# Branch projections by seven products on half-size blocks, with the two sides of PSUM exchanged

## The chip, the cores and the metric

The kernel runs on one core of one Trainium2 chip. The metric is the device time of one execution in microseconds (us), lower is better. A profiled execution also has a span, from its first instruction to its last.

## What is computed

One step of a hybrid decoder layer for 512 prompt tokens and 32 sample tokens (544 columns in all), in fp32. Three branches work on the projected input: a short convolution, a state-space recurrence, a cross-attention. What matters here is how they are merged:

```python
conv_out = (cb * conv * jax.nn.silu(cz)) @ p['w_conv_out']
...
ys = jax.nn.gelu(ys * jax.nn.silu(sz))
ssm_out = (ys @ p['w_glu_a']) * jax.nn.sigmoid(ys @ p['w_glu_b'])
...
attn_out = (o * jax.nn.silu(az)) @ p['w_attn_out']
g = jax.nn.sigmoid(gpre).reshape(bsz, L, N_BRANCH, D_MODEL)
merged = g[:, :, 0] * conv_out + g[:, :, 1] * ssm_out + g[:, :, 2] * attn_out
return x + merged @ p['w_out'], new_conv, new_re, new_im
```

The four matrices `w_attn_out`, `w_conv_out`, `w_glu_a` and `w_glu_b` are 1024 x 2048 each. The four products with them, each of 1024 x 2048 by 1024 x 544, are the branch projections, and they are all that the change rewrites.

## The kernel before, in words

Activations lie transposed: channels on the 128 partitions, the T = 544 tokens along the free dimension, in two halves of NH = 272. A matrix product in fp32 is made of three products in the faster format F32R: every operand is split into a high part `hi` (a copy on ScalarE, ACT, L91) and a low part `lo` (source minus high part, on VectorE, DVE, L92), and hi*hi, hi*lo and lo*hi are summed in PSUM. The helper `split` (L90 to L92) records both instructions, so most splits of the kernel have these two lines in the profile and differ by their tiles.

The plain product is `proj` (L127). It takes 256 columns of a weight matrix through `stream` (L94), which loads blocks of 512 rows by 256 columns (512 KB, queue of SyncE, SP; pool `wraw`, four buffers), splits each (pool `whl`, two buffers), and issues 48 matmuls per block: 2 column tiles of 128, 4 row tiles, 3 products, 2 halves of the tokens. With 1024 rows a call has 2 blocks and 96 matmuls. After each block `tick` runs a step of background work, if there is any.

The stage ahead of the branches computes the gates (L1059 to L1066) with `winograd` (L1009): Winograd's form of Strassen's algorithm. The weights are halved along rows and columns and the activations along channels and tokens, and seven products of halves take the place of eight. The blocks of weights that go into the products are sums and differences: three on DVE (L1038, L1045, L1048), one on GpSimd (POOL, L1044). The blocks of activations, the factors `XT`, are made and split once, in the stage before. A product is 24 matmuls; its split weights lie in `shi` and `slo` with three buffers each. Results are added up partly in PSUM (products that accumulate on an earlier one) and partly on DVE (L1050, L1052, L1055). The gates go to DRAM (`gt_d`), by POOL's queue.

The branch stage (L1070 to L1122) first opens the standard pools again (`open_std`, L1070), then loads the three branch inputs from DRAM (`od_d`, `cv_d`, `gz_d`) with `branch_input` (L1081): eight pieces of 272 KB by ACT's queue, each split on arrival into `preh` and `prel`. Then come three loops over 8 groups of 256 columns. For attention, DVE multiplies the result out of PSUM with the gate into `mg` (L1102). For the convolution, DVE multiplies (L1108) and POOL adds to `mg` (L1109). For the GLU there are two `proj` calls per group, a sigmoid on ACT (L1118), two multiplications on DVE (L1114, L1119) and POOL's addition (L1120). Gates are loaded by ACT's queue (L1093).

After it (L1128) the sixteen tiles `mg` are split into `mh` and `ml` and multiplied with `w_out`, in the same manner with `proj`.

Order on the engines: the program is recorded in the order of the code, and the Tile framework then orders each engine's instructions by its own schedule (the `TileContext` of the launch has `schedule_with_timeline_sim=True`), so an instruction can run ahead of earlier code when its inputs are there. In the gate stage the difference L1045 of one call runs ahead of the addition L1055 of the call before. Each engine then works its list in order. A pool with `reuse_waits="tile"` lets a new tile wait for just those older tiles whose memory it takes.

## Time and profile before

| | us |
|---|---|
| median of 3 runs | 2225.22 |
| the runs | 2224.7 to 2228.82 |
| the profiled execution's own time | 2227.26 |
| its span | 2225.5 |
| TensorE matmuls busy | 2126.1 |
| DVE busy | 1107.5 |
| ACT busy | 708.8 |
| POOL busy | 481.3 |

PE is TensorE's matmul, PEld its weight load, which overlaps it. Matmuls are pipelined, so a matmul's own duration (some 0.29 us) is longer than the time from one start to the next. "mean ns" is the mean duration of one instruction; "idle before" is time in which the engine waited ahead of these instructions, with what released it. Lines as L92 are lines of the kernel.

### The profile page before, as it was taken

Reading aid. Unit: us, or ns where it says so; the run is one execution under the profiler, and the core shown is the slowest. Engines: PE = TensorE matmul, PEld = TensorE weight load, DVE = VectorE, ACT = ScalarE, POOL = GpSimd, SP = SyncE. Lnnn points to the kernel's source line nnn. Section 1 sums busy time; section 2 is a strip of 40 time slices with the busy share of each in tenths; the row PEclk is TensorE's granted clock in tenths of the full one; section 3 lists DMA queues with packets and bytes.
Section 4 is the critical chain, followed back from the end, with each engine's and each line's share of the span. In section 5 each row is a group of like instructions: output and inputs, shape, how many; then the busy total and the mean of one; then the engine's idle time right before and its main releaser. Section 6 shows DMA issues by size and latency. Waiting matters only on the chain.

```text
span 2225.5 us, 39522 instructions
## 1 busy us (share of the span) xinstructions
PE 2126.1 (96%) x16962; PEld 2095.3 (94%) x16962; DVE 1107.5 (50%) x1623; ACT 708.8 (32%) x1014; POOL 481.3 (22%) x336
## 2 busy tenths in 40 slices
PE   3989999999999999989899999999899999999996
PEld 3989999999999998889799999999899999999996
DVE  4534598423334443266567677677544433334232
ACT  4122221223233333223344444444322112223332
POOL 0198510740100002144212111111000210011221
PEclk9999999999999999999899999999999999999998
DMA  6565133344243445543333333334454433327232
GB/s 140 123 126 107 59 96 96 109 109 130 87 143 125 132 162 176 176 145 107 107 126 129 121 124 134 126 125 134 163 190 146 136 121 120 106 86 178 84 96 81
DMA packets 262483, 277.00 MB, mean 124 GB/s; under 512 B 59146, under 2 KB 242018, under 8 KB 260292
## 3 DMA queue, kind: packets, MB, share of 16 engines
q1 hardware_dynamic: 214144, 204.11, 30.9%
q10 hardware_dynamic: 39460, 37.62, 6.0%
q0 software_dynamic: 8704, 32.75, 4.0%
q8 instruction: 133, 2.18, 0.4%
q14 instruction: 42, 0.34, 0.1%
HBM read 241.96 MB, written 31.96 MB: 123 GB/s over the span
## 4 chain that ended last, share of the span: by engine, by line
PE 76%; DVE 5%; DMA 2%; issue 1%; ACTq 1%; ACT 1%; POOL 0%; DVEq 0%; SPq 0%; POOLq 0%
PE mmps L137 15%; PE mmps L143 15%; PE mmps L140 15%; PE pA L1032 13%; PE pB L1032 9%; PE mmps L824 1%; PE mmps L823 1%; PE mmps L825 1%; DVE wlo L92 1%; PE aux L618 1%; PE aux L875 1%; PE dsc L863 1%; DMA stage<-od_d 1%; PE aux L779 1%; PE aux L616 1%
## 5 line engine op out<-in xcount | busy, mean ns | idle before, releaser
L92 DVE TENSOR_TENSOR wlo<-raw,whi 128x1024 fp32r<-128x1024 f32 x256 | 351.2, 1373 | 594.7 <-ACT whi L91 583.5
L91 ACT ACTIVATE whi<-raw 128x1024 fp32r<-128x1024 f32 x256 | 271.2, 1060 | 841.3 <-PE mmps L140 726.7
L143 PE MATMUL mmps<-xh,wlo 128*128 128x272 f32 x2048 | 428.8, 291 | 10.7 <-DVE wlo L92 10.5
L137 PE MATMUL mmps<-xh,whi 128*128 128x272 f32 x2048 | 431.7, 292 | 3.1 <-DVE gate L980 2.2
L140 PE MATMUL mmps<-xl,whi 128*128 128x272 f32 x2048 | 430.7, 290 | 0.0
L143 PEld LDWEIGHTS mmps<-xh,wlo 128*128 128x128 f32 x2048 | 322.7, 189 | 18.3 <-DVE wlo L92 12.4
L140 PEld LDWEIGHTS mmps<-xl,whi 128*128 128x128 f32 x2048 | 325.9, 190 | 4.2 <-issue 4.1
L137 PEld LDWEIGHTS mmps<-xh,whi 128*128 128x128 f32 x2048 | 322.8, 190 | 6.0 <-DVE gate L980 2.4
L92 DVE TENSOR_TENSOR slo<-sraw,shi 128x1024 fp32r<-128x1024 f32 x120 | 191.2, 1593 | 83.0 <-ACT shi L91 83.0
L137 PE MATMUL mmps<-preh,whi 128*128 128x272 f32 x1024 | 213.9, 291 | 10.0 <-ACT preh L91 7.9
L140 PE MATMUL mmps<-prel,whi 128*128 128x272 f32 x1024 | 212.8, 289 | 0.5 <-DVE prel L92 0.5
L143 PE MATMUL mmps<-preh,wlo 128*128 128x272 f32 x1024 | 210.7, 288 | 0.0
L91 ACT ACTIVATE shi<-sraw 128x1024 fp32r<-128x1024 f32 x120 | 126.9, 1058 | 168.0 <-PE pA L1032 83.1
L137 PEld LDWEIGHTS mmps<-preh,whi 128*128 128x128 f32 x1024 | 160.8, 189 | 10.9 <-ACT preh L91 8.6
L140 PEld LDWEIGHTS mmps<-prel,whi 128*128 128x128 f32 x1024 | 162.6, 190 | 1.1 <-DVE prel L92 1.1
L143 PEld LDWEIGHTS mmps<-preh,wlo 128*128 128x128 f32 x1024 | 160.4, 189 | 0.0
L1044 POOL TENSOR_TENSOR sraw<-sraw 128x1024 f32<-128x1024 f32 x24 | 77.1, 3214 | 290.6 <-DVE sum L1038 287.9
L1032 PE MATMUL pA<-xh,shi 128*128 128x272 f32 x384 | 112.2, 292 | 9.0 <-ACT shi L91 9.0
L1032 PE MATMUL pA<-xh,slo 128*128 128x272 f32 x384 | 112.2, 292 | 1.4 <-DVE slo L92 1.4
L1032 PE MATMUL pA<-xl,shi 128*128 128x272 f32 x384 | 111.7, 291 | 0.0
L1032 PE MATMUL pB<-xh,shi 128*128 128x272 f32 x384 | 111.0, 289 | 0.0
L1032 PE MATMUL pB<-xh,slo 128*128 128x272 f32 x384 | 110.9, 289 | 0.0
(367 smaller groups left out, 4039.0 us busy)
## 6 DMA issues: line engine op xcount, KB each, us to landing
raw<-in_w_in_dram SPq DMA_DIRECT2D x128, 512.0 KB, 3.5
sraw<-in_w_in_dram SPq DMA_DIRECT2D x96, 512.0 KB, 3.6
raw<-in_w_out_dram SPq DMA_DIRECT2D x32, 512.0 KB, 3.4
gt_d<-sgate POOLq DMA_DIRECT2D x24, 544.0 KB, 3.0
gate<-gt_d ACTq DMA_DIRECT2D x24, 544.0 KB, 3.8
raw<-in_w_mem_k_dram SPq DMA_DIRECT2D x16, 512.0 KB, 3.8
raw<-in_w_mem_v_dram SPq DMA_DIRECT2D x16, 512.0 KB, 3.4
kb<-in_cache_mem_k_dram POOLq DMA_DIRECT2D x8, 1024.0 KB, 5.4
```

The lines of the kernel that those rows point to most:

```text
L91: S.activation(hi, src, AF.Copy)
L92: V.tensor_sub(lo, src, hi.bitcast(F32))
L137: nc.tensor.matmul(ps[m][:, n, :NH], lh, rh(kt, n), start=(kt == 0), stop=False)
L140: nc.tensor.matmul(ps[m][:, n, :NH], lh, rl(kt, n), start=False, stop=False)
L143: nc.tensor.matmul(ps[m][:, n, :NH], ll, rh(kt, n), start=False, stop=(kt == nk - 1))
L616: nc.tensor.matmul(py[:, q * 72:(q + 1) * 72], mt[:, g * 128:(g + 1) * 128], U[:, g0 + g, 0:72], start=True, stop=False)
L618: nc.tensor.matmul(py[:, q * 72:(q + 1) * 72], ctw[:, g * 128:(g + 1) * 128], Sb[:, 0:72, g0 + g], start=False, stop=True)
L779: nc.tensor.matmul(scv, a[:, dt, lt * 128:(lt + 1) * 128], b[:, dt, :], start=(i == 0), stop=(i == 5))
L823: nc.tensor.matmul(o, lh, hi[:, q, :], start=(kt == 0), stop=False)
L824: nc.tensor.matmul(o, lh, lo[:, q, :], start=False, stop=False)
L1032: nc.tensor.matmul(ps, a[:, k, :], t[:, k, :], start=new and i == 0, stop=i == 23, skip_group_check=not new)
L1044: P.tensor_sub(a21, a11, a21)
```

## The change

The three loops over 256 columns become loops over 4 groups of 512 columns, each with one call of `winograd2` (two for the GLU). `winograd2` takes 1024 rows and 512 columns of weights in four blocks of 512 by 256 (`blk`, five buffers), forms the seven products (each 2 column tiles by 4 row tiles by 3, 24 matmuls with 272 moving columns), splits their weights into `bhi` and `blo` (two buffers each), and adds up in four PSUM banks (`pbA`, `pbB`) and on DVE. It writes whole results into SBUF, so the gates are then multiplied SBUF by SBUF, four tiles per call.

The activations' factors are made in `factors_of` and `finish_factors`, three per chunk in the background (`tick`, twice per call) and four at once ahead of the phase. They have one buffer each, two for factors 1, 5 and 6. Branch inputs come in four loads of 544 KB. The small PSUM pool `aux` moves to the right side, since the new pools take the left; `open_std` moves behind the branch stage.

```diff
--- before.py
+++ after.py
@@ -42,7 +42,7 @@
         const = ctx.enter_context(tc.tile_pool(name="const", bufs=1))
         small = ctx.enter_context(tc.tile_pool(name="small", bufs=6))
         dram = ctx.enter_context(tc.tile_pool(name="dram", bufs=1, space=DRAM))
-        aux = ctx.enter_context(tc.tile_pool(name="aux", bufs=4, space=PSUM))
+        aux = ctx.enter_context(tc.tile_pool(name="aux", bufs=4, space=PSUM, side="right"))
         ws = {}
         def open_std():
@@ -1067,59 +1067,166 @@
         sts.close()
         xts.close()
         xs.close()
-        open_std()
-        pre_s = ExitStack()
-        prp = pre_s.enter_context(tc.tile_pool(name="prp", bufs=2, side="right", reuse_waits="tile"))
+        brs = ExitStack()
+        fcp = brs.enter_context(tc.tile_pool(name="fcp", bufs=1, side="right", reuse_waits="tile"))
         mgs = ExitStack()
         mgp = mgs.enter_context(tc.tile_pool(name="mgp", bufs=1, reuse_waits="tile"))
         mg = [mgp.tile([128, T], F32, name=f"mg{j}") for j in range(16)]
         bps = ExitStack()
-        bp = bps.enter_context(tc.tile_pool(name="bp", bufs=2, reuse_waits="tile"))
-        def branch_input(src):
-            h = prp.tile([128, 8, T], F32R, name="preh")
-            l = prp.tile([128, 8, T], F32R, name="prel")
-            for ct in range(8):
-                st = bp.tile([128, T], F32, name="stage", bufs=4)
-                S.dma_start(out=st, in_=src[ct * 128:(ct + 1) * 128, :])
-                split(h[:, ct, :], l[:, ct, :], st)
-            return (lambda kt, n: h[:, kt, n * NH:(n + 1) * NH]), (lambda kt, n: l[:, kt, n * NH:(n + 1) * NH])
-        def gate(br, jp):
-            sg = bp.tile([128, 2, T], F32, name="gate", bufs=3)
-            S.dma_start(out=sg, in_=gt_d[br, jp])
-            return sg
...
+        bp = bps.enter_context(tc.tile_pool(name="bp", bufs=1, reuse_waits="tile"))
+        pbA = bps.enter_context(tc.tile_pool(name="pbA", bufs=2, space=PSUM, reuse_waits="tile"))
+        pbB = bps.enter_context(tc.tile_pool(name="pbB", bufs=2, space=PSUM, reuse_waits="tile"))
+        def factor(F, n):
+            F[n] = tuple(fcp.tile([128, 4, NH], F32R, name=f"b{hl}{n}", bufs=2 if n in (1, 5, 6) else 1)
+                         for hl in "hl")
+            return F[n]
+        def factors_of(src, F):
+            bk = []
+            for c in range(2):
+                b = []
+                for kh in range(2):
+                    t = bp.tile([128, 2, T], F32, name="big", bufs=6)
+                    r0 = (4 * kh + 2 * c) * 128
+                    S.dma_start(out=t, in_=src[r0:r0 + 256, :].rearrange("(k p) t -> p k t", p=128))
+                    b.append(t)
+                bk.append((b[0][:, :, :NH], b[0][:, :, NH:], b[1][:, :, :NH], b[1][:, :, NH:]))
+            yield
+            for n in (1, 5, 6):
+                factor(F, n)
+            rest = []
+            for c, (b11, b12, b21, b22) in enumerate(bk):
+                k2 = slice(2 * c, 2 * c + 2)
+                split(F[1][0][:, k2], F[1][1][:, k2], b11)
+                P.tensor_sub(b11, b12, b11)
+                yield
+                split(F[5][0][:, k2], F[5][1][:, k2], b11)
+                P.tensor_sub(b12, b22, b12)
+                yield
+                P.tensor_sub(b11, b22, b11)
+                split(F[6][0][:, k2], F[6][1][:, k2], b11)
+                yield
+                rest.append((k2, b11, b12, b21, b22))
+            F["rest"] = rest
+        def finish_factors(F):
+            for n, i in ((3, 4), (7, 2), (2, 3), (4, None)):
+                h, l = factor(F, n)
+                for r in F["rest"]:
+                    if i is None:
+                        P.tensor_sub(r[3], r[3], r[1])
+                    split(h[:, r[0]], l[:, r[0]], r[i or 3])
+        def winograd2(w, col0, F, o):
+            blk = {}
+            for kh, mh_ in ((0, 1), (1, 1), (0, 0), (1, 0)):
+                t = blk[mh_, kh] = bp.tile([128, 4, 256], F32, name="blk", bufs=5)
+                nc.sync.dma_start(out=t, in_=w[kh * 512:kh * 512 + 512, col0 + 256 * mh_:col0 + 256 * mh_ + 256]
+                                  .rearrange("(k p) n -> p k n", p=128))
+            a11, a12, a21, a22 = blk[0, 0], blk[0, 1], blk[1, 0], blk[1, 1]
+            def product(ps, n, src, new):
+                hi = bp.tile([128, 4, 256], F32R, name="bhi", bufs=2)
+                lo = bp.tile([128, 4, 256], F32R, name="blo", bufs=2)
+                split(hi, lo, src)
+                th, tl = F[n]
+                for s in range(2):
+                    i = 0
+                    for k in range(4):
+                        for a, t in ((hi, th), (hi, tl), (lo, th)):
+                            nc.tensor.matmul(ps[s], a[:, k, s * 128:(s + 1) * 128], t[:, k, :],
+                                             start=new and i == 0, stop=i == 11, skip_group_check=not new)
+                            i += 1
+            bank = lambda pool, nm: [pool.tile([128, 512], F32, name=nm)[:, :NH] for _ in range(2)]
+            t0, t1 = slice(0, NH), slice(NH, T)
+            s1 = bp.tile([128, 4, 256], F32, name="bsum")
+            pa = bank(pbA, "pbA")
+            V.tensor_add(s1, a21, a22)
+            product(pa, 1, a11, True)
+            for s in range(2):
+                S.copy(o[s][:, t0], pa[s])
+            pb = bank(pbB, "pbB")
+            product(pb, 5, s1, True)
+            for s in range(2):
+                S.copy(o[2 + s][:, t1], pb[s])
+            P.tensor_sub(a21, a11, a21)
+            V.tensor_sub(a11, s1, a11)
+            product(pa, 6, a11, False)
+            for s in range(2):
+                S.copy(o[s][:, t1], pa[s])
+            V.tensor_sub(s1, a12, a11)
+            product(pb, 3, s1, False)
+            for s in range(2):
+                V.tensor_add(o[s][:, t1], pb[s], o[s][:, t1])
+            product(pa, 7, a21, False)
+            for s in range(2):
+                V.tensor_add(o[2 + s][:, t1], pa[s], o[2 + s][:, t1])
+            pc = bank(pbB, "pbB")
+            product(pc, 2, a12, True)
+            for s in range(2):
+                V.tensor_add(o[s][:, t0], pc[s], o[s][:, t0])
+            tick()
+            product(pa, 4, a22, False)
+            for s in range(2):
+                S.copy(o[2 + s][:, t0], pa[s])
+            tick()
+        def gate(br, q):
+            out = []
+            for i in range(2):
+                sg = bp.tile([128, 2, T], F32, name="big", bufs=6)
+                S.dma_start(out=sg, in_=gt_d[br, 2 * q + i])
+                out += [sg[:, 0, :], sg[:, 1, :]]
+            return out
+        def outs():
+            return [bp.tile([128, T], F32, name="bo", bufs=4) for _ in range(4)]
+        rate[0] = 1
+        Fa, Fc, Fz = {}, {}, {}
+        for _ in factors_of(od_d, Fa):
+            pass
+        finish_factors(Fa)
+        bg.append(factors_of(cv_d, Fc))
+        for q in range(4):
+            winograd2(w_attn_out[0], q * 512, Fa, mg[4 * q:4 * q + 4])
+            sg = gate(2, q)
+            for m in range(4):
+                V.tensor_mul(mg[4 * q + m], mg[4 * q + m], sg[m])
+        tick(1000)
+        finish_factors(Fc)
+        bg.append(factors_of(gz_d, Fz))
+        for q in range(4):
+            o = outs()
+            winograd2(w_conv_out[0], q * 512, Fc, o)
+            sg = gate(0, q)
+            for m in range(4):
+                V.tensor_mul(o[m], o[m], sg[m])
+                P.tensor_add(mg[4 * q + m], mg[4 * q + m], o[m])
+        tick(1000)
+        finish_factors(Fz)
+        for q in range(4):
+            o = outs()
+            winograd2(w_glu_a[0], q * 512, Fz, o)
+            sg = gate(1, q)
+            for m in range(4):
+                V.tensor_mul(sg[m], o[m], sg[m])
+            o = outs()
+            winograd2(w_glu_b[0], q * 512, Fz, o)
+            for m in range(4):
+                S.activation(o[m], o[m], AF.Sigmoid)
+                V.tensor_mul(sg[m], sg[m], o[m])
+                P.tensor_add(mg[4 * q + m], mg[4 * q + m], sg[m])
         bps.close()
-        pre_s.close()
+        brs.close()
         mhp = ctx.enter_context(tc.tile_pool(name="mhp", bufs=1, side="right", reuse_waits="tile"))
@@ -1128,6 +1235,7 @@
         for j in range(16):
             split(mh[j], ml[j], mg[j])
         mgs.close()
+        open_std()
         fin = ctx.enter_context(tc.tile_pool(name="fin", bufs=1, reuse_waits="tile"))
         yt = [fin.tile([128, D], F32, name=f"yt{i}") for i in range(5)]
         def mrh(kt, n):
```

## Rows read from the trace of the kernel before

**Rows 1.** The page: busy us, share of the span, instructions by engine.

```profile
PE 2126.1 (96%) x16962; PEld 2095.3 (94%) x16962; DVE 1107.5 (50%) x1623; ACT 708.8 (32%) x1014; POOL 481.3 (22%) x336
```

**Rows 2.** Busy time by stretch: branch stage, its steady part, the gate stage.

```profile
core 0: us, PE busy (x) PEld busy (x) DVE busy (x) ACT busy (x) POOL busy (x), PEclk, DMA share, GB/s
1605.00:2003.00 398.00, 390.93 (x3075) 389.38 (x3076) 148.99 (x152) 92.41 (x106) 42.52 (x31) 0.99 0.42 135
1730.00:1830.00 100.00, 100.00 (x799) 100.00 (x798) 41.15 (x34) 17.87 (x18) 19.08 (x14) 1.00 0.40 128
1400.00:1500.00 100.00, 100.00 (x800) 100.00 (x799) 72.26 (x64) 44.88 (x61) 19.10 (x10) 1.00 0.38 130
```

**Rows 3.** Chain that ended last: start, us, what; one product.

```profile
1102.70 3.01 PE pB L1032 x24
```

**Rows 4.** Tile preh: duration ns min/median/max, first and last start.

```profile
L137 PE MATMUL mmps<-preh,whi x1024: 284/288/596, 1605.7 to 1999.9; 128*128 128x272 f32 x171
```

**Rows 5.** Groups by line, DVE, gate stage: busy us, mean ns, idle before.

```profile
L92 DVE TENSOR_TENSOR slo<-sum,shi 128x1024 fp32r<-128x1024 f32 x46 | 56.2, 1221 | 13.5 <-ACT shi L91 13.2
L1038 DVE TENSOR_TENSOR sum<-sraw 128x1024 f32<-128x1024 f32 x23 | 28.2, 1226 | 26.5 <-DMA sraw<-in_w_in_dram 26.5
L1050 DVE TENSOR_TENSOR sgate<-pB,sgate 128x272 f32<-128x272 f32 x24 | 10.6, 442 | 21.1 <-PE pB L1032 21.1
```

**Rows 6.** Groups by line, 1605 to 2003.

```profile
L91 ACT ACTIVATE whi<-raw 128x1024 fp32r<-128x1024 f32 x64 | 67.9, 1060 | 271.6 <-PE mmps L140 266.6 <-DMA gate<-gt_d 5.0
L92 DVE TENSOR_TENSOR prel<-stage,preh 128x544 fp32r<-128x544 f32 x24 | 16.7, 721 | 18.4 <-ACT preh L91 18.2
L1119 DVE TENSOR_TENSOR gate<-gate,sb 128x544 f32<-128x544 f32 x16 | 11.6, 722 | 12.8 <-ACT sb L1118 12.8
```

**Rows 7.** Timeline, gate stage, DVE and POOL: start, us, engine, line.

```profile
1213.63 1.22 DVE L92 TENSOR_TENSOR slo<-sraw,shi 128x1024 fp32r<-128x1024 f32 x1
1214.77 0.43 DVE L1052 TENSOR_TENSOR sgate<-pA,sgate 128x272 f32<-128x272 f32 x1
1215.12 3.07 DVE L92 TENSOR_TENSOR slo<-sraw,shi 128x1024 fp32r<-128x1024 f32 x1
...
1213.86 3.25 POOL L1044 TENSOR_TENSOR sraw<-sraw 128x1024 f32<-128x1024 f32 x1 [11.06 <-DVE sum L1038]
```

**Rows 8.** Timeline, branch stage, POOL and DVE.

```profile
1748.30 1.36 POOL L1109 TENSOR_TENSOR mg<-mg,gate 128x544 f32<-128x544 f32 x1 [1.66 <-DVE gate L1108]
...
1748.34 2.40 DVE L92 TENSOR_TENSOR wlo<-raw,whi 128x1024 fp32r<-128x1024 f32 x1
```

**Rows 9.** Waits, 1100 to 1600: us in total, times, longest.

```profile
ACT shi L91 <- PE pA L1032: 106.1, 66, 2.0
ACT shi L91 <- PE pB L1032: 105.5, 69, 1.7
DVE slo L92 <- ACT shi L91: 95.8, 68, 1.8
```

**Rows 10.** Busy time by stretch, start of the branch stage.

```profile
1600.00:1606.00 6.00, 0.33 (x1) 0.33 (x2) 0.35 (x1) 0.70 (x2) 0.53 (x1) 0.68 0.94 251
1606.00:1627.00 21.00, 16.55 (x107) 15.23 (x107) 10.30 (x15) 8.73 (x14) 0.00 (x0) 0.91 0.80 287
```

**Rows 11.** Timeline, ACT and its queue, start of the branch stage.

```profile
1599.66 1.78 ACTq L1087 DMA_DIRECT2D stage<-od_d  x4
...
1604.96 0.66 ACT L91 ACTIVATE preh<-stage 128x544 fp32r<-128x544 f32 x1 [4.92 <-DMA stage<-od_d]
```

**Rows 12.** Timeline, PE, end of the branch stage.

```profile
2000.26 0.41 PE L143 MATMUL mmps<-preh,wlo 128*128 128x272 f32 x2
2002.63 0.78 PE L137 MATMUL mmps<-mh,whi 128*128 128x272 f32 x4 [1.95 <-ACT mh L91]
```

**Rows 13.** DMA issues, 1605 to 2003: KB each, median us to landing.

```profile
raw<-in_w_glu_a_dram SPq DMA_DIRECT2D x16, 512.0 KB, 3.6
```

More of the change, by code (lines that the diff above doesn't have):

```diff
@@ L1091, in gate @@
-        def gate(br, jp):
-            sg = bp.tile([128, 2, T], F32, name="gate", bufs=3)
-            S.dma_start(out=sg, in_=gt_d[br, jp])
-            return sg
-        pat = branch_input(od_d)
-        pcv = branch_input(cv_d)
-        for jp in range(8):
-            sg = gate(2, jp)
-            ps = proj(w_attn_out[0], jp * 256, *pat, 8)
-            for m in range(2):
-                V.tensor_mul(two(mg[2 * jp + m]), ps[m], two(sg[:, m, :]))
-        pgz = branch_input(gz_d)
-        for jp in range(8):
-            sg = gate(0, jp)
-            ps = proj(w_conv_out[0], jp * 256, *pcv, 8)
-            for m in range(2):
-                V.tensor_mul(two(sg[:, m, :]), ps[m], two(sg[:, m, :]))
-                P.tensor_add(mg[2 * jp + m], mg[2 * jp + m], sg[:, m, :])
@@ L1110, in hybrid_step_kernel @@
-        for jp in range(8):
-            sg = gate(1, jp)
-            psa = proj(w_glu_a[0], jp * 256, *pgz, 8)
-            for m in range(2):
-                V.tensor_mul(two(sg[:, m, :]), psa[m], two(sg[:, m, :]))
-            psb = proj(w_glu_b[0], jp * 256, *pgz, 8)
-            for m in range(2):
-                sb = bp.tile([128, T], F32, name="sb", bufs=3)
-                S.activation(two(sb), psb[m], AF.Sigmoid)
-                V.tensor_mul(sg[:, m, :], sg[:, m, :], sb)
-                P.tensor_add(mg[2 * jp + m], mg[2 * jp + m], sg[:, m, :])
+        bp = bps.enter_context(tc.tile_pool(name="bp", bufs=1, reuse_waits="tile"))
```

## The prediction

> **What bounds the kernel now.** I read the shares of the engines first: TensorE's matmuls fill 96% of the span, VectorE half of it [rows 1]. Then the table by stage [rows 2]. The branch projections that the change rewrites run from about 1605 to 2003 us, and in their steady part 799 matmuls start in 100 us, at clock 1.00 with no gap: 125.2 ns from one to the next. VectorE is busy there for 41 of 100 us and POOL for 19. So this stage is bound by the number of matmuls. The stage before it, the gates, already works by seven products; 800 matmuls in 100 us, so that form costs the same per matmul (24 of them, one product, take 3.01 us [rows 3]), but VectorE is busy for 72 of 100 us. What the change costs must be read from that stage.
>
> **What is removed.** The first matmul of the branch stage starts at 1605.7 [rows 4] and the last at about 2000.4: 394.7 us for 3072 matmuls (32 calls of `proj` by 96), of which 384.6 are their pitch and some 10 are gaps near the start. After: 16 calls of `winograd2`, each 7 products by 24, so 2688. 384 fewer by 125.2 ns are **-48.1 us**. The Trainium skill (TensorE: Matmul & The Clock Gate, "Wait — 56ns, not 53.3ns?") gives columns over 2.4 GHz and some 2.5 ns more, an estimate of 116 ns for 272 columns and of -44.5 us for the sum; the trace has 125.2, and I keep it.
>
> **What is added on VectorE and POOL.** Per call of `winograd2` (512 columns of weights, 168 matmuls, 21.03 us of TensorE): 7 splits whose low half takes VectorE 1.22 us, 3 sums or differences of blocks at 1.225, 6 additions out of PSUM at 0.44 [rows 5], 4 products with the gates at 0.722 [rows 6]. That is 8.54 + 3.68 + 2.65 + 2.89 = 17.8 us. Before, the same columns cost 4 splits and 4 products from PSUM, about 8 us.
>
> POOL counts too, since the two exclude each other. In [rows 7] POOL's subtraction of 1024 elements runs from 1213.86 to 1217.11; the split that VectorE starts at 1215.12 lasts 3.07 us instead of 1.22 and ends 1.08 us after POOL does. The addition from PSUM at 1214.77 keeps its 0.43 in the middle of it. POOL itself got in only when VectorE's earlier split ended at 1214.85, so it holds the way for 2.26 us. The 544-element addition of `mg` does the same: POOL 1.36 us, the split beside it 2.40, end again 1.08 later [rows 8]. Every VectorE instruction with both inputs in SBUF therefore adds to every POOL instruction. Per call, without the additions from PSUM: 15.1 + 2.26 = 17.4; with them 20.0. Then by phase:
> - attention: next factors in the background, 6 splits at 0.72 [rows 6] and 6 POOL subtractions at 1.36 over 4 calls, +3.1: 20.5 to 23.1;
> - convolution: the same, and 4 POOL additions per call, +5.4: 25.9 to 28.6;
> - the two GLU products: POOL additions in every second call, on average +2.7: 20.1 to 22.7.
>
> VectorE's instructions overlap by 0.08 us (1.22 long, next start after 1.14 [rows 7]), some 20 per call: 1.6 less in each. So attention 18.9 to 21.5, convolution 24.3 to 27.0, GLU 18.5 to 21.1, against 21.03 of TensorE. The low end holds if POOL always runs beside an addition from PSUM, the high end if never. On top, `finish_factors` ahead of the convolution and of the GLU: 8 splits and 2 subtractions, 8.5 us each.
>
> **What that costs TensorE.** Little can be saved up: factors `bhi` and `blo` have two buffers, so product i+2 can't be split before product i ends. ACT's half takes 1.06 [rows 6], VectorE's 1.22; together 2.3 of the 3.0 us that product i+1 gives (its first two matmuls need no low half, 0.25 more): 0.9 us of room. In the gate stage, with three buffers, ACT already waits 135 times for the release [rows 9]. At a call's end work bunches: two gate products become ready after the copy of product 4, then two POOL additions, then the difference a11 with its split. From the start of the next product 1: gate products at 0.75 and 1.4, one POOL addition to 3.3, the split of product 5 to 4.5 where 3.25 was free, then the difference, ACT's half and the split of product 6 to about 9.2 where 7.65 was: some 3.5 us lost, counting part of the last addition.
> - Convolution: demand in mid range, 25.6, is 4.6 over; 4 calls 18.5, and half of `finish_factors`, 4: 22.5.
> - GLU: 3.5 in each of 4 calls with POOL additions, 0.7 in the others, and 4 for `finish_factors`: 21.
> - Attention: 1.5 in each of three calls; the first is in the start: 4.5.
>
> Sum **+48 us**; bounds 13 (only the convolution's 3.3 per call) and 82 (convolution 6 per call and all of `finish_factors`, 4 in every GLU call, 3 in attention).
>
> **Start.** Now the gate stage's last matmul ends near 1600.0, and to 1606 there is nothing for TensorE, then 107 matmuls in 21 us where 168 fit [rows 10]; the first loads of `od_d` are issued at 1599.66 and used at 1604.96 [rows 11]. Against pitch 15.6 us are lost in all. After: the same bytes in four larger loads, 14 splits and 8 POOL subtractions (10.1 + 10.9 us) beside the first call's own 20: some 33 us from about 1609 on, after the first landing and a part of the work. That ends the first call near 1643, 22 us late: **+7**; bounds 0 (the larger loads land sooner) and 15. The weights of this stage now lie in new buffers, without the splits that ran ahead of 1600; that is in the 7.
>
> **End.** `open_std` moves behind the branches, so the first `w_out` blocks wait for its place in SBUF, partly where `mg` lay. Now TensorE idles about 2 us there [rows 12]. Nearest row taken: **+1.5**; bounds -1 (twelve of sixteen `mg` are final earlier and can be split ahead) and 8 (a load of 3.6 us [rows 13], a split and a slower clock).
>
> Edits at nothing: the side of PSUM (no transfer, same 8 banks; 0 either way, as `aux` keeps its four); the weight loads (same 64 by 512 KB in the same shape; five buffers for four blocks, of which the first comes free near the third product, 3.6 us of load against some 10 us of room; if a later one were waited for it would be 3 us per call). ACT has 7 by 1.06, 8 copies under 0.5 and in half of the GLU calls four sigmoids, below 15 of 21 us.
>
> **Sum:** -48.1 + 48 + 7 + 1.5 = +8.4 us. It is made on the profiled execution (span 2225.5, its own time 2227.26); the three runs have their median at 2225.22, so 2.0 of the 2227.26 is that one run, and I add to the median: **2233.6 us**.
>
> **Rivals.**
> 1. *TensorE stays the bound* (the other side). POOL runs in gaps that VectorE has anyway while it waits for ACT: in the gate stage 95.8 us of such waits in 500 [rows 9]. Stalls of 20 (convolution 13, the rest 7), start +4, end +1: -48.1 + 25 = -23, **2202**. It decides if demand in the GLU calls stays under 21.03. For it: the gate stage loses nothing at 72% VectorE. Against it: there one POOL instruction per call, here up to seven, and two buffers instead of three.
> 2. *Two buffers are the bound.* The 0.9 us of room go at nearly every product, to a copy of ACT or a block sum of 1.225 that stands before the split. 0.7 us for each of 112 products is 78 in place of 48: **2263**. The Trainium skill (Perfetto Trace Analysis, "Optimization Strategy") says that a gap repeated on the engine that should be saturated can mean too few buffers; no row before shows such gaps with two, since a block of `proj` is twice as long as a product.
> 3. *Gain and stalls cancel* within the bound below: stalls of 40, **2225**.
> That the products aren't really fewer I give no chance: the loops count 168.
>
> **Chances.** Forecast 0.45 (its own range 2222 to 2246), rival 1 0.33, rival 2 0.12, rival 3 0.10. About 0.2% (4.5 us) is what a measurement of this kernel can tell from no change. Faster: 0.34 (rival 1 and a sliver of the forecast); same: 0.15 (rival 3 and 0.05 of the forecast); slower: 0.51. The range takes in rival 1 down to stalls near its bound (13: -48.1 + 13 + 4 = -31) and rival 2 with a bad start: 2195 to 2272.
>
> **What would show it.** Right: about 2688 matmuls in the stage; VectorE and POOL together near 20 us per call in attention and GLU and above 24 in the convolution; splits of 2.4 to 3.1 us beside POOL; TensorE waiting for `blo`, most in the convolution. Wrong: if the stage's matmuls keep 125 ns through the GLU calls (rival 1), if ACT's half waits for TensorE at every product while VectorE idles (rival 2), or if TensorE waits for loads of `blk`.

## The result and the profile after

The changed kernel takes **2323.55 us** (median of 4 runs, 2323.01 to 2330.35), the kernel before beside it 2227.02: a ratio of **1.043 [1.0407, 1.0453]**. It is slower, as forecast, but by some 96 us where 8 were forecast, and outside the range.

First the page of the kernel after: busy time, share of the span and instructions of each engine, as in [rows 1].

```profile
span 2321.7 us, 39332 instructions
PE 2107.0 (91%) x16578; PEld 2064.0 (89%) x16578; DVE 1336.7 (58%) x1833; ACT 811.1 (35%) x1208; POOL 597.0 (26%) x376
```

TensorE has 384 matmuls fewer, just as worked out (16962 in [rows 1]), and yet its share falls from 96% to 91%. So it waits, and the question is where. The table below cuts both executions at the same four events: the last matmul of the gates, the first and the last matmul of the branches, the first matmul with `w_out`.

| profiled execution | before | after | difference |
|---|---|---|---|
| up to the last gate matmul | 1599.5 | 1603.3 | +3.8 |
| wait at the start of the branches | 6.2 | 19.6 | +13.4 |
| branch stage, first to last matmul | 394.8 | 430.1 | +35.3 |
| idle before the first `w_out` matmul | 2.1 | 46.1 | +44.0 |
| rest | 222.9 | 222.6 | -0.3 |
| span | 2225.5 | 2321.7 | +96.2 |

The first line is not the change's: that event fell between 1598.4 and 1608.0 in the executions of all the kernels below, which share the program up to there. Three places remain. The table by stage of the kernel after shows them (columns as in [rows 2]); its lines are the wait at the start, the first call of `winograd2`, the other attention calls, the convolution, the GLU, the idle time at the end, and the whole stage.

```profile
1603.00:1623.00 20.00, 0.55 (x5) 0.32 (x3) 4.88 (x4) 4.05 (x7) 4.47 (x4) 0.57 0.94 315
1623.00:1667.00 44.00, 30.97 (x164) 28.38 (x165) 42.84 (x37) 18.73 (x30) 30.34 (x14) 0.77 0.32 99
1667.00:1735.00 68.00, 64.28 (x503) 63.12 (x502) 56.11 (x62) 33.22 (x51) 7.19 (x3) 1.00 0.45 141
1735.00:1850.00 115.00, 92.17 (x670) 87.59 (x669) 100.48 (x94) 47.77 (x74) 52.37 (x24) 0.97 0.40 131
1850.00:2053.00 203.00, 179.44 (x1358) 174.02 (x1356) 169.70 (x167) 89.56 (x137) 55.98 (x26) 0.97 0.29 95
2053.00:2099.00 46.00, 0.13 (x2) 0.00 (x0) 13.81 (x19) 10.83 (x19) 9.73 (x3) 0.54 0.66 146
1623.00:2053.00 430.00, 366.86 (x2688) 353.11 (x2688) 369.14 (x357) 189.28 (x291) 145.87 (x67) 0.96 0.35 112
```

Against the whole-stage line of [rows 2], VectorE went from 149 busy us to 369 and POOL from 43 to 146. In the first call and the convolution VectorE is busy for 97% and 87% of the time. In the 46 us at the end no engine is: that is a wait for something else. By calls (168 matmuls, 21.03 us at pitch, each counted up to the start of its last matmul), the three attention calls behind the first took 68.4 us, the convolution's 34.9, 27.3, 26.4, 27.0, and the GLU's in turn (a, b, a, b ...) 30.9, 23.0, 28.8, 22.1, 27.3, 21.2, 27.0, 21.2. The b calls, which have only gate products ahead of them, lose 2 us at most; the a calls, which run beside POOL's additions of the call before them, lose 6 to 10.

**The end.** SyncE's queue, then POOL, DVE and TensorE at the end of the branch stage, kernel after (start, us, engine, line, what; in brackets the idle time before and its releaser):

```profile
2069.36 11.77 SPq L215 DMA_DIRECT2D yt<-in_x_prompt_dram  x8
2081.17 29.06 SPq L98 DMA_DIRECT2D raw<-in_w_out_dram  x7
...
2061.34 6.20 POOL L1227 TENSOR_TENSOR mg<-mg,big 128x544 f32<-128x544 f32 x1 [4.48 <-DVE big L1226]
...
2061.19 5.16 DVE L92 TENSOR_TENSOR ml<-mg,mh 128x544 fp32r<-128x544 f32 x8
2068.26 0.72 DVE L92 TENSOR_TENSOR ml<-mg,mh 128x544 fp32r<-128x544 f32 x1 [1.92 <-ACT mh L91]
...
2099.09 0.82 PE L137 MATMUL mmps<-mh,whi 128*128 128x272 f32 x2 [45.96 <-ACT whi L91]
```

Read from the bottom. TensorE waited 45.96 us (1.95 in [rows 12]) for the first split block of `w_out`. Its load was issued at 2081.17, because the place of `open_std`'s buffers was free only when the sixteen `mg` had been split, and because eight loads of `yt` stand before it in SyncE's queue, waiting for the same place. That place came free late as well: the last `ml` split ran at 2068.26, held up by the last addition to `mg`, which took POOL 6.20 us instead of the 1.36 of [rows 8]. VectorE had begun eight splits in a row just before it (2061.19 to 2066.35), and POOL ended 1.19 us after them. The chain of waits adds what the transfers cost; the first `w_out` block took 16.73 us to land beside the others, where a block of the branch stage before took 3.6 [rows 13]:

```profile
2067.57 0.67 ACT mh L91
2068.26 0.74 DVE ml L92
...
2070.53 10.11 DMA yt<-in_x_prompt_dram
...
2081.17 16.73 DMA raw<-in_w_out_dram
```

**The start.** POOL, SyncE's queue, ACT and VectorE, kernel after, against [rows 10, 11]:

```profile
1604.15 0.53 POOL L1066 DMA_DIRECT2D gt_d<-sgate  x1 [18.99 <-ACT sgate L1063]
...
1611.62 3.43 SPq L1131 DMA_DIRECT2D blk<-in_w_attn_out_dram  x5
...
1617.43 0.66 ACT L91 ACTIVATE bh<-big 128x544 fp32r<-128x544 f32 x1 [13.58 <-DMA blk<-in_w_attn_out_dram]
...
1618.12 0.73 DVE L92 TENSOR_TENSOR bl<-big,bh 128x544 fp32r<-128x544 f32 x1 [17.23 <-ACT bh L91]
```

The first block of weights is asked for at 1611.62, right after the last store of the gates (issued at 1604.15) has landed at 1611.48, and it lands at 1616.99. In the kernel before, SyncE's queue asked for such blocks from 1573.37 on, 26 us before the gates ended. VectorE begins with the factors at 1618.12. TensorE starts at 1622.9, and the first call then takes 44.6 us.

### The profile page after: what moved, and what is told of

The parts are those of the page before. It is cut to its first block, busy times and chain, and to the rows that moved or that the text cites. A ratio compares the mean times of both kernels' runs of the same rounds, so it can differ in the third digit from the quotient of the medians.

```text
span 2321.7 us, 39332 instructions
## 1 busy us (share of the span) xinstructions
PE 2107.0 (91%) x16578; PEld 2064.0 (89%) x16578; DVE 1336.7 (58%) x1833; ACT 811.1 (35%) x1208; POOL 597.0 (26%) x376
## 4 chain that ended last, share of the span: by engine, by line
PE 65%; DVE 12%; issue 3%; DMA 3%; ACT 1%; ACTq 1%; POOL 1%; SPq 0%; DVEq 0%; POOLq 0%
PE pA L1032 13%; PE pB L1032 9%; PE mmps L143 9%; PE mmps L137 9%; PE mmps L140 8%; PE pbA L1144 5%; DVE blo L92 4%; PE pbB L1144 3%; PE mmps L824 1%; PE mmps L823 1%; PE mmps L825 1%; DVE wlo L92 1%; DVE bl L92 1%; ACT bhi L91 1%; PE aux L618 1%
## 5 line engine op out<-in xcount | busy, mean ns | idle before, releaser
L92 DVE TENSOR_TENSOR wlo<-raw,whi 128x1024 fp32r<-128x1024 f32 x192 | 265.7, 1385 | 480.9 <-ACT whi L91 477.3
L143 PEld LDWEIGHTS mmps<-xh,wlo 128*128 128x128 f32 x2048 | 324.0, 190 | 19.3 <-DVE wlo L92 13.4
L1144 PE MATMUL pbA<-bh,bhi 128*128 128x272 f32 x512 | 149.1, 295 | 29.2 <-ACT bhi L91 28.3
L1144 PE MATMUL pbA<-bh,blo 128*128 128x272 f32 x512 | 146.5, 302 | 26.9 <-DVE blo L92 26.7
L1144 PE MATMUL pbA<-bl,bhi 128*128 128x272 f32 x512 | 149.1, 295 | 2.3 <-DVE bl L92 2.3
L92 DVE TENSOR_TENSOR blo<-blk,bhi 128x1024 fp32r<-128x1024 f32 x80 | 137.6, 1720 | 12.7 <-ACT bhi L91 12.5
L137 PE MATMUL mmps<-mh,whi 128*128 128x272 f32 x448 | 95.0, 294 | 46.0 <-ACT whi L91 46.0
L1144 PEld LDWEIGHTS pbA<-bh,bhi 128*128 128x128 f32 x512 | 99.5, 195 | 31.0 <-ACT bhi L91 29.3
L1144 PEld LDWEIGHTS pbA<-bh,blo 128*128 128x128 f32 x512 | 96.2, 194 | 34.6 <-DVE blo L92 34.5
L1144 PE MATMUL pbB<-bh,blo 128*128 128x272 f32 x384 | 107.8, 301 | 20.5 <-DVE blo L92 20.5
L1144 PE MATMUL pbB<-bl,bhi 128*128 128x272 f32 x384 | 112.0, 296 | 3.5 <-DVE bl L92 3.5
```

Of the source, the lines that this page charges most:

```text
L92: V.tensor_sub(lo, src, hi.bitcast(F32))
L137: nc.tensor.matmul(ps[m][:, n, :NH], lh, rh(kt, n), start=(kt == 0), stop=False)
L143: nc.tensor.matmul(ps[m][:, n, :NH], ll, rh(kt, n), start=False, stop=(kt == nk - 1))
L1144: nc.tensor.matmul(ps[s], a[:, k, s * 128:(s + 1) * 128], t[:, k, :], start=new and i == 0, stop=i == 11, skip_group_check=not new)
```

## The experiments

All kernels compute the whole reference; they move buffers, queues or engines. Names of the form "idle" and "wait" mean the columns of the table above.

**x1: the end, the queue.** The loads of `yt` and `fg` are recorded behind the first `w_out` product:

```diff
-        for i in range(5):
-            load_rows(yt[i], i)
...
-        S.dma_start(out=fg, in_=final_norm_g.partition_broadcast(128))
...
+            if jp == 0:
+                for i in range(5):
+                    load_rows(yt[i], i)
+                S.dma_start(out=fg, in_=final_norm_g.partition_broadcast(128))
```

> The residual's loads (yt, fg) are recorded behind the first product with w_out instead of ahead of it; nothing else changes. Theory Q (order on SyncE's queue): in the changed kernel TensorE idles 46 us at the end of the branches because the w_out blocks stand behind eight yt loads, which wait for the last mg split, and then share the memory with them; with the order reversed the first w_out block can be issued as soon as the first two mg tiles are split, near 2056, and the idle time falls to about 10 us, the kernel to about 2288. Rival M (memory alone): the w_out blocks themselves wait for mg tiles that are final last; then the first load starts at about 2069 all the same, lands in 5 us, the idle time is 22 to 25 us and the kernel near 2300. If it stays above 2318, neither.

2298.81 us, 1.0303 [1.0264, 1.0341]. The idle time falls from 46.1 to 16.8, between the two expectations; the rest grows by 4.6, since `yt` now comes late. SyncE's queue, POOL, ACT and TensorE in the timeline of this kernel:

```profile
2058.56 5.92 SPq L98 DMA_DIRECT2D raw<-in_w_out_dram  x4
2062.42 6.20 POOL L1227 TENSOR_TENSOR mg<-mg,big 128x544 f32<-128x544 f32 x1 [4.47 <-DVE big L1226]
2069.76 1.06 ACT L91 ACTIVATE whi<-raw 128x1024 fp32r<-128x1024 f32 x1 [0.45 <-issue]
2070.87 0.82 PE L137 MATMUL mmps<-mh,whi 128*128 128x272 f32 x2 [16.66 <-ACT whi L91]
```

The first `w_out` block is now asked for at 2058.56, before the last `mg` is split. So the order in the queue, and what goes with it, is worth 29 of the 44 us. What is left is no load: ACT turns to `whi` only behind its sixteen `mh` splits, and the last of these waits for POOL's 6.20 us.

**b_late: the end alone, in the kernel before.** The standard pools get the lifetime that the change gives them, and nothing else is touched: opened above `mg` for the branches, closed, and opened again where the change opens them.

```diff
-        open_std()
...
+        open_std()
         bps = ExitStack()
...
         pre_s.close()
+        ws["st"].close()
...
         mgs.close()
+        open_std()
```

> The kernel before, with eight products as it was; only the place of the standard pools is moved: they are opened above mg for the branches, closed, and opened again behind the splits of mg, as in the changed kernel. Theory M (the idle time at the end comes from where and when the w_out blocks get their memory and their turn on SyncE's queue, not from the seven products): the idle time ahead of the first matmul with w_out grows from 2 us to 30 to 45 us here too, and the kernel comes to 2255 to 2275. Rival T (it is the changed kernel's crowded VectorE and POOL at the end): it stays under 12 us.

2271.81 us, 1.019 [1.0158, 1.0222]. Branch stage 398.5, wait at the start 7.2, rest 221.9, and the idle time goes from 2.1 to 41.0, with the same order in SyncE's queue (timeline, queue of SyncE and TensorE):

```profile
2016.98 10.33 SPq L215 DMA_DIRECT2D yt<-in_x_prompt_dram  x8
2027.36 79.09 SPq L98 DMA_DIRECT2D raw<-in_w_out_dram  x15
...
2045.03 0.82 PE L137 MATMUL mmps<-mh,whi 128*128 128x272 f32 x2 [40.80 <-ACT whi L91]
```

The end term is shown by itself, without any winograd product in the branches.

**x4: the place of the blocks.** The buffers `blk` get a pool of their own below `mg`, in place that the stage before leaves free early:

```diff
+        bks = ExitStack()
+        bkp = bks.enter_context(tc.tile_pool(name="bkp", bufs=1, reuse_waits="tile"))
...
-                t = blk[mh_, kh] = bp.tile([128, 4, 256], F32, name="blk", bufs=5)
+                t = blk[mh_, kh] = bkp.tile([128, 4, 256], F32, name="blk", bufs=5)
```

> The weight blocks blk get a pool of their own below mg, so that they lie where the gate stage's raw weights lay and not where its last gate tiles lie. Theory S (the first weight load of the branches waits for the store of the last gate tile, 1604 to 1611, and then takes 5.4 us): the loads run ahead of 1603, the first matmul of the branches comes near 1612 instead of 1622.9, and the kernel gains 8 to 11 us: about 2313. Rival C (ACT's queue is held by the issue of a cv_d load that waits for an earlier transfer, and that wait is the one that ends last): the first matmul moves by less than 4 us and so does the time.

2282.94 us, 1.0231 [1.0171, 1.0292]. The wait at the start goes from 19.6 to 9.9, as the place predicts: SyncE's queue asks for the first block at 1580.44, well before the gates have ended. The idle time at the end falls too, to 17.6, which I hadn't expected: the buffers of `open_std` now lie over `blk`, whose places come free one after another in the last call, and not over `mg`, so that the first `w_out` block is asked for at 2022.32, ahead of `yt`. SyncE's queue at the start and at the end, then ACT, in this kernel's timeline:

```profile
1580.44 53.27 SPq L1133 DMA_DIRECT2D blk<-in_w_attn_out_dram  x6
...
2022.32 20.58 SPq L98 DMA_DIRECT2D raw<-in_w_out_dram  x4
2056.39 16.76 SPq L215 DMA_DIRECT2D yt<-in_x_prompt_dram  x8
...
2060.73 0.66 ACT L91 ACTIVATE mh<-mg 128x544 fp32r<-128x544 f32 x1 [5.25 <-POOL mg L1229]
2062.58 2.00 ACT L91 ACTIVATE whi<-raw 128x1024 fp32r<-128x1024 f32 x2 [1.19 <-DMA yt<-in_x_sample_dram]
```

So the order of the two in the queue can be had by place as well as by the order of the code. What is left is on ACT (the last two lines): as in x1, `whi` comes behind the last `mh`, which waits for POOL's addition.

**x5: the crowd of the first call.** The background work on the convolution's input starts one call later:

```diff
-        bg.append(factors_of(cv_d, Fc))
...
+            if q == 0:
+                bg.append(factors_of(cv_d, Fc))
```

> The background work for the convolution's factors is begun after the first attention call instead of ahead of it. Theory C (ACT's queue stands 13 us behind the issue of a cv_d load that waits for an earlier transfer): the first split of od_d runs near 1610 and the first call ends 6 us or more earlier, kernel near 2312. Rival S (the first weight block, which waits for the last gate store, is what ends last): the first matmul stays near 1622.9; what is gained is only the cv_d factor work beside the first call, 2 to 5 us.

2318.94 us, 1.0401 [1.0373, 1.043]. The wait stays 19.5: those loads are not what delays it. The first call ends 62.1 us after the gates instead of 64.2, at the low end of rival S.

**x2: POOL's arithmetic.** All of POOL's additions and subtractions in the branch stage (L1107, L1110, L1112, L1123, L1160, L1213, L1227) go to VectorE; one of the seven lines:

```diff
-            P.tensor_sub(a21, a11, a21)
+            V.tensor_sub(a21, a11, a21)
```

> All arithmetic of the branch stage that POOL does (a21, the additions to mg, the differences of the factors) is put on VectorE; VectorE gets 16 more instructions of 1024 and 56 of 544 elements. Theory L (POOL and VectorE exclude each other, their sum is the bound): a VectorE instruction costs 1.14 or 0.64 us where POOL holds the way 2.26 or 1.36 and more, so the stage loses 16 x 1.1 + 56 x 0.7 = 57 us of demand, and of the 70 us that TensorE stalls after the first call some 25 to 45 go: 2280 to 2300. Rival G (POOL's work runs in gaps, the two buffers are the bound): VectorE gets 54 us more work and nothing less, and the kernel is slower, 2335 or more.

2272.56 us, 1.0185 [1.0146, 1.0224], lower than theory L had it. The branch stage falls from 430.1 to 386.2, 37 of it behind the first call and so within the 25 to 45 given; the rest comes at the start, at the end and ahead of the stage. The stage by busy time, and VectorE's low split, of this kernel (the second from 1657 on):

```profile
1620.00:2006.00 386.00, 357.78 (x2688) 345.96 (x2686) 334.96 (x425) 189.15 (x291) 0.00 (x0) 0.98 0.40 126
...
L92 DVE TENSOR_TENSOR blo<-blk,bhi 128x1024 fp32r<-128x1024 f32 x75 | 91.6, 1222 | 8.6 <-ACT bhi L91 8.6
```

In the kernel after, the groups by line from 1600 to 2110 were:

```profile
L92 DVE TENSOR_TENSOR blo<-blk,bhi 128x1024 fp32r<-128x1024 f32 x80 | 137.6, 1720 | 12.7 <-ACT bhi L91 12.5
L1160 POOL TENSOR_TENSOR blk<-blk 128x1024 f32<-128x1024 f32 x16 | 41.3, 2584 | 200.4 <-ACT bhi L91 41.8 <-DMA blk<-in_w_glu_b_dram 33.5 <-DMA blk<-in_w_glu_a_dram 31.4
L1227 POOL TENSOR_TENSOR mg<-mg,big 128x544 f32<-128x544 f32 x16 | 36.5, 2281 | 43.2 <-DVE big L1226 43.2
L1226 DVE TENSOR_TENSOR big<-big,bo 128x544 f32<-128x544 f32 x16 | 21.7, 1358 | 0.8 <-ACT bo L1225 0.8
```

VectorE does 68 instructions more in this stage (x425 against x357) and is busy for less time, 335 us against 369. The same split takes 1.22 us in the mean instead of 1.72. POOL's work was not beside VectorE's but inside it, and longer there than on VectorE itself.

**x2b: a part of it.** Only the 32 additions to `mg` (L1213, L1227) go to VectorE.

> The changed kernel with nothing but POOL's 32 additions to mg on VectorE; a21 and the factors' differences stay on POOL. Theory L with work bunched at a call's end: the calls of the convolution and those that follow a GLU call with additions lose most of their stalls, about 25 of the 44 us that all of POOL's work made, and the 6.2 us addition at the end is gone: 2290 to 2297. If the subtractions of 1024 elements weigh more, less than 15 us: above 2306.

2303.93 us, 1.0339 [1.032, 1.0358]. The branch stage falls by 15.8 and the idle time at the end by 4.6, with the addition of 6.20 us gone. Between the two cases that I had set out: the additions are 16 of the 44 us. By difference the subtractions (a21 and the factors') have the larger share; they were not moved by themselves.

**x3: three buffers.**

```diff
-                hi = bp.tile([128, 4, 256], F32R, name="bhi", bufs=2)
-                lo = bp.tile([128, 4, 256], F32R, name="blo", bufs=2)
+                hi = bp.tile([128, 4, 256], F32R, name="bhi", bufs=3)
+                lo = bp.tile([128, 4, 256], F32R, name="blo", bufs=3)
```

> Three buffers in place of two for bhi and blo. Theory L: demand on VectorE and POOL is the same, so little changes; a few of the stalls at a call's start go, at most 10 us: 2313 to 2323. Rival B (two buffers are the bound): ACT no longer waits for the product before last, the 70 us of stalls fall by half or more: below 2290.

2296.65 us, 1.0293 [1.0255, 1.0331]: the branch stage falls by 25.3, more than the one theory gave and less than the other. The waits for the release of `bhi`, and TensorE's for the low half, first in the kernel after (1667 to 2053; last TensorE's for the high half), then with three buffers (1667 to 2028; us in total, times, longest):

```profile
ACT bhi L91 <- PE pbA L1144: 64.0, 52, 3.4
ACT bhi L91 <- PE pbB L1144: 55.7, 37, 3.1
...
PE pbA L1144 <- DVE blo L92: 24.8, 29, 1.9
...
PE pbB L1144 <- DVE blo L92: 16.9, 10, 3.5
...
PE pbA L1144 <- ACT bhi L91: 7.9, 2, 5.9
```

```profile
ACT bhi L91 <- PE pbA L1144: 46.4, 29, 3.2
ACT bhi L91 <- PE pbB L1144: 42.0, 25, 3.3
```

The waits fall from 89 to 54 in number. The two buffers are not the bound by themselves, but a third lets the bursts be spread. Calls 2 to 16, which lose 70 us in the kernel after, lose 45 here, 33 in x2 and 23 in x_all below, which has both edits and more: the two gains overlap and aren't to be added.

**b_aux: the side of PSUM.** In the kernel before, `aux` alone goes to the right side.

```diff
-        aux = ctx.enter_context(tc.tile_pool(name="aux", bufs=4, space=PSUM))
+        aux = ctx.enter_context(tc.tile_pool(name="aux", bufs=4, space=PSUM, side="right"))
```

> The kernel before with the small PSUM pool aux on the right side, nothing else. Priced at nothing: within 0.2% of the kernel before. Rival: if the banks' order matters, the whole kernel shifts, by 4 us or more (the changed kernel reaches the end of the gate stage 3.8 us later than the kernel before).

2230.25 us, 0.9996 [0.9982, 1.001]: nothing, as in the prediction.

**x_all: the edits together.** x1, x2, x3, x4 and x5 in one kernel.

> All edits on the changed kernel at once: the residual's loads behind the first w_out product, POOL's work of the branch stage on VectorE, three buffers for bhi and blo, blk below mg, the cv_d factors begun one call later. If the parts add up (44 us from POOL's work, 10 or more from the third buffer on top of it, 12 at the start, 35 to 40 at the end), the kernel comes to 2205 to 2220, at or a little below the kernel before. If the end is held by the chain of mg splits whatever the loads do, some 2225 to 2235.

2222.76 us against 2231.64 of the kernel before, 0.9968 [0.9953, 0.9983]. The time lies between the two cases expected. The branch stage takes 369.8 us, 25.0 less than in the kernel before; the wait is 9.9 and the idle time 11.2.

**x_low3 and x_low3_early: the remaining 11 us at the end.** x_low3 also puts `bhi` and `blo` into the low pool, so that the split buffers of `w_out` come free early, and loads the prompt's rows of `yt` by POOL's queue; x_low3_early records these loads early again, still on POOL's queue.

```diff
-                hi = bp.tile([128, 4, 256], F32R, name="bhi", bufs=3)
+                hi = bkp.tile([128, 4, 256], F32R, name="bhi", bufs=3)
...
-                    load_rows(yt[i], i)
+                    load_rows(yt[i], i, P)
```

> x_all with two more edits: bhi and blo lie in the low pool too, below mg, so that the first w_out block can be loaded and split before mg is split; and the residual's loads go by POOL's queue, so that no w_out block stands behind them. If the idle time at the end (11.2 us in x_all) hangs on the place of the buffers, it falls to 3 to 6 us, and the w_out stage is back from 228.8 us to about 223: some 2205 to 2213, 0.5 to 1% below the kernel before. If it hangs on the splits of mg alone, 2215 to 2222.

> The same, with the residual's loads recorded ahead of the first w_out product, where the changed kernel has them, but by POOL's queue. If it was their place in SyncE's queue that held the w_out blocks, and not the memory bandwidth they take, the time is that of x_low3 within 4 us. If bandwidth counts, the first w_out blocks land late and it is 6 to 12 us slower.

2221.09 us, 0.9961 [0.9946, 0.9976], and 2222.43 us, 0.9964 [0.9952, 0.9976]. Early or late makes no difference here, but the pair doesn't tell queue from bandwidth as I had meant it to: POOL's queue asks for the first `yt` 0.3 us after the last matmul of the branches in both (1984.28 and 1986.15), whatever the order of the code. First x_low3, then x_low3_early:

```profile
1984.57 1.05 POOL L215 DMA_DIRECT2D yt<-in_x_prompt_dram  x2 [379.00 <-PE pbA L1146]
```

```profile
1986.44 1.05 POOL L215 DMA_DIRECT2D yt<-in_x_prompt_dram  x2 [379.62 <-PE pbA L1146]
```

So how the loss at the end of the kernel after divides between the turn in the queue and the transfers themselves (16.73 us for the first `w_out` block, beside `yt`) is not shown. And the idle time stayed at 10.4 where I had expected it nearly gone. SyncE's queue and ACT in the timeline of x_low3:

```profile
1958.40 41.08 SPq L98 DMA_DIRECT2D raw<-in_w_out_dram  x6
...
1988.99 4.48 ACT L91 ACTIVATE mh<-mg 128x544 fp32r<-128x544 f32 x8
1993.38 1.99 ACT L91 ACTIVATE whi<-raw 128x1024 fp32r<-128x1024 f32 x2
```

The first block of weights was asked for 35 us before ACT split it. It waited behind ACT's own row of `mh` splits: an order on an engine, not a load.

**x_first: that order turned.** The branches and `w_out` share one pair of pools that stays open (`raw` with five buffers, `hl` with three), and the sixteen `mg` are split four at a time, each four ahead of the `w_out` block that needs them:

```diff
+        def split_mg(b):
+            for j in range(4 * b, 4 * b + 4):
+                split(mh[j], ml[j], mg[j])
...
+        ps0 = proj(w_out[0], 0, mrh, mrl, 16, split_mg)
+        mgs.close()
...
-            ps = proj(w_out[0], jp * 256, mrh, mrl, 16)
+            ps = proj(w_out[0], jp * 256, mrh, mrl, 16) if jp else ps0
```

> x_low3 with the order at the end changed: the pools for raw and split weights are the same tiles for the branches and for w_out, below mg, and the splits of mg are recorded four at a time ahead of the w_out block that needs them, so that ACT splits the first w_out block before it has split all of mg. In x_low3 TensorE idles 10.4 us there although the first w_out block was asked for 22 us earlier. If that idle time is the order on ACT, it falls to 3 to 5 us and the kernel to 2210 to 2216; if VectorE's chain of products, additions and splits holds it, no more than 3 us are gained.

**2210.02 us against 2228.63 of the kernel before, 0.9921 [0.9908, 0.9935]**: this version beats both kernels. The wait at the start is 5.4, the branch stage 370.7, the idle time 2.0; TensorE's timeline at the end:

```profile
1982.30 0.77 PE L139 MATMUL mmps<-mh,whi 128*128 128x272 f32 x4 [1.85 <-ACT mh L91]
```

That is the line of [rows 12] again, 20 us earlier. Of the gain on x_low3 8.4 us come at the end, more than expected, and 6.2 at the start, where none was expected (the wait was 11.6 there); the branch stage is 2.4 longer. Of the 48.1 us of matmuls saved, 24.1 arrive in the branch stage; the rest is still lost, in the first call and four others (below).

## Why the prediction was right in its sign and wrong in its size

Its four terms were -48.1 + 48 + 7 + 1.5 = +8.4 us; measured, they are -48.1 + 70 + 26.8 + 44 = +92.7. The 3.8 of the gate stage and the -0.3 of the rest make up the 96.2 of the table. The sign doesn't hang on the two ends: with the forecast 7 and 1.5 in their place the sum is still +30.

**Removed: right.** 2688 matmuls in the stage, 384 fewer at the same pitch.

**TensorE stalls (+48, bounds 13 to 82): right mechanism, undersized; measured +70.** Calls 2 to 16 took 385.5 us where 15 by 21.03 are 315.5. The step's rule, that an instruction of VectorE with both inputs in SBUF and one of POOL add to one another, holds. In x2 the moved instructions take 57 us on VectorE (16 at 1.225, 52 at some 0.72), so that without them it would be busy 278; in the kernel after it is busy 369. The 91 us between are POOL's 67 instructions, 1.36 each; by the step's 1.36 and 2.26 they'd be some 105. Attention came out at 5.3 (forecast 4.5). What failed is the size of a burst: "some 3.5 us lost" in each GLU call with additions, "4.6 over" in a convolution call. Behind the first of each they measured 6.0 to 7.8 and 5.4 to 6.3, and the first calls, which have `finish_factors` ahead of them, 9.9 and 13.9 instead of 7.5 and 8.6. The step had priced half of `finish_factors` as hidden. GLU 33.3 (forecast 21), convolution 31.5 (forecast 22.5). That the additions and subtractions on POOL are behind the larger part of it is shown by x2 (44 us less, of which 6.9 in the first call), that they are more than a matter of average load by x3 (25 us for a third buffer).

**Start (+7, bounds 0 to 15): wrong; measured +26.8.** The first call ends 64.2 us after the gates, so 43.2 late; 16.4 of it were lost before too (15.6 in the prediction). "The same bytes in four larger loads" was the wrong thing to look at. The step put "the weights of this stage now lie in new buffers" into the 7 without a price. Its own work of 10.1, 10.9 and 20 us is 41, of which it let 8 be done by 1609 without a row for it; VectorE had done none of it before 1618.12. 13.4 of the excess is the longer wait before the first matmul; by place alone x4 takes 9.7 away, and x_first has no excess left. The other 13.4 is the first call itself: VectorE is busy for 42.84 of 44 us there. x5 moved 2.1 of it, and x2, with POOL empty, shortened the call by 6.9; how the rest divides between the factors and the low clock (0.77 in that stretch) was not tried.

**End (+1.5, bounds -1 to 8): wrong, and the largest miss; measured +44.** The step set 1.5 by the "nearest row", and let an opened pool cost 8 at most: a load of 3.6 us, a split and a slower clock. It asked where the place lies but not which loads stand before it in the queue: eight of `yt`, ready at the same moment as the place itself. Nor did it see what the old place had given, namely that the blocks were loaded during the branches: in the kernel before the queue asked for `w_out` from 1972.66 on, 28 us before the branches ended. b_late shows the whole term in the kernel before (+39), x1 what the order in the queue is worth (29), x_first that what is left behind it goes with ACT's order, in a run that also shares the buffers and has more of them.

**Edits at nothing: right** for the side of PSUM (b_aux). The weight loads were free in the middle of the stage (from 1667 to 2053 TensorE has no wait for `blk`); their place cost at its start.

**The rivals.** 1, TensorE stays the bound, asked for a demand under 21.03 us in the GLU calls. VectorE was busy for 169.70 us in the eight, its waits for POOL included: 21.2 a call. So the condition was just missed, by 1.5 us over eight calls, where TensorE lost 33. With the same work and a third buffer (x3) the eight calls lose 15: the bursts weigh more than the mean.

2, two buffers are the bound, is half right. TensorE's waits are for VectorE's low half (41.7 us) far more than for ACT's high half (7.9), and VectorE didn't idle meanwhile (busy for 84 to 87% of the GLU and the convolution); but ACT waited for a release 89 times in the 105 products of calls 2 to 16, a third buffer gives back 25 us, and the stalls, 70, are nearer to its 78 than to the forecast's 48. The Trainium skill (Perfetto Trace Analysis, "Optimization Strategy"), by which a repeated gap on the engine that should be saturated can mean too few buffers, pointed the right way for those 25 us.

3, gain and stalls cancel, holds for no version here before the other edits are made: even with POOL empty (x2) the ends decide. x_all is near it, 0.9968.

In x_first the branch stage still takes 370.7 us where its matmuls need 336.5. Its trace says where: first the GLU's first call, then nearly all of the seven behind it (columns as in [rows 2]):

```profile
1808.00:1835.00 27.00, 23.63 (x171) 22.74 (x170) 26.04 (x35) 10.92 (x18) 0.00 (x0) 0.94 0.59 203
1835.00:1980.00 145.00, 145.00 (x1160) 145.00 (x1159) 125.44 (x155) 75.00 (x118) 0.00 (x0) 1.00 0.36 114
```

Behind its first call the GLU runs at pitch, with VectorE busy for 87% of the time. The loss lies in five calls: 33.4 us for the first of all and 24.7 for the second, 25.6 and 27.6 for the convolution's first two, 27.0 for the GLU's first, where factors are being made or have just been finished. What of it is their work on VectorE and what the slower clock behind the gaps (0.94 in the first line), no run takes apart.

## What to carry to other kernels

When an edit moves the opening of a pool, price three things: which memory it takes and who frees that last, which loads stand ahead of its own in the same queue, and what was loaded ahead of time in the old place; a block's own 3.6 us was the smallest of them here. When arithmetic is given to POOL beside a VectorE that works from SBUF, compare its cost inside VectorE's time with the cost on VectorE itself. A stage that loads a second engine nearly as much as the first is judged by its bursts and buffers too: here the GLU lost a sixth of its time with VectorE busy for 84% of it, and nothing behind its first call at 87%, with POOL empty and a third buffer.

## What was unexpected of the hardware

POOL doesn't always get the next turn beside VectorE. Mostly it does, as the prediction had it from [rows 7]: it waits for the VectorE instruction under way, and the next one waits for POOL, though VectorE has no gap. So here in the kernel after (POOL, then VectorE):

```profile
1910.65 2.27 POOL L1227 TENSOR_TENSOR mg<-mg,big 128x544 f32<-128x544 f32 x1 [0.66 <-DVE big L1226]
...
1910.49 1.21 DVE L92 TENSOR_TENSOR blo<-bsum,bhi 128x1024 fp32r<-128x1024 f32 x1
1911.63 1.87 DVE L1226 TENSOR_TENSOR big<-big,bo 128x544 f32<-128x544 f32 x1
```

But the last addition of 1.36 us took 6.20 when VectorE had eight splits ready in a row, and ended 1.19 us after the last of them; twice (kernel after and x1) to the same hundredth. Among POOL's 72 instructions from 1600 to 2070 us one more was kept out like that, a subtraction of 544 elements at 1737.74 that took 5.89 us, past six VectorE instructions. What decides who goes next is open. The Trainium skill (SBUF — State Buffer, "Who interferes with whom") calls the port pair that the two share an exclusive lock, for which a VectorE instruction with two inputs in SBUF contends with a GpSimd instruction that reads SBUF. The trace agrees on the exclusion: the addition above and the VectorE instruction behind it take 2.27 and 1.87 us instead of 1.36 and 0.72.

And an engine can be relieved by giving it more work: with POOL's 68 instructions on VectorE, VectorE's busy time in the branch stage fell by 34 us and the kernel's time by 51.
